# Mixer input, mixer weights and attention tiles moved to one place mod 256 bytes

## The chip, the cores and the metric

The kernel runs on one core of one Trainium2 chip. The metric is the device time of one execution in microseconds. The time before is 871.11 us, the median of 3 runs (870.56 to 871.52).

## The reference

One decoder layer on x of 512 tokens by 1024 features, float32:

```
h = RMSNorm(x)
[q | k | v | x_rnn | g_rnn | gate_attn | gate_rnn] = h @ W_in      (seven blocks of 1024 columns)
A = differential attention(q, k, v)    8 heads, two maps of 64 features each, v of 128, causal,
                                       q and k normalised, a bias by relative distance
R = GeLU(g_rnn) * RG-LRU(CausalConv4(x_rnn))
x = x + (sigmoid(gate_attn) * (A @ P_attn) + sigmoid(gate_rnn) * (R @ P_rnn)) @ W_out
x = x + relu(RMSNorm(x) @ W_up)^2 @ W_down                         (4096 hidden features)
```

## The kernel before

**Three products for one.** Every large product is done on TensorE in the type float32r, with each operand split into a high part and the rest. `mm3` (lines 135 to 138) issues three matmuls: high x high, high x low, low x high. Each has its own weight load (LDWEIGHTS) of the standing operand, 128 columns; the moving operand streams 512 or 256 columns. The traces list these three as L136, L137 and L138.

**Two shapes.** Feature-major products (`cols_proj`) hold weights as the standing operand and stream 512 tokens of an activation; one unit of weights, 4 x 128 rows by 256 columns, gives 24 matmuls. The gates, x_rnn, g_rnn, the attention's and the recurrent branch's projections, W_out and W_up are done this way. Token-major products (`tok_proj`) hold 128 tokens of the activation `hT` as the standing operand and stream 256 weight columns; q, k and v are done this way, 1152 matmuls in all. The down projection (line 1153) also streams 256 columns: the squared-ReLU activations `us` are moving, the weights standing.

**Where operands lie.** A place here is the address of an operand's first element within its partition, mod 256 bytes. The steps that a product takes inside a tile (128 or 256 or 512 columns of 4 bytes) are multiples of 256 bytes, so a tile's place is that of all its pieces. The places follow from the allocation of the pools, in the order of the code:

| operand | tile and pool | place before |
|---|---|---|
| h, split (`hT`) | one tile of the pool `hp`, left side | 64 |
| h before its norm, split (`hu`), used by the first gate units | pool `p1` | 128 |
| weights `whi`, `wlo` | pool `wp`, buffers of 1024 + 64 elements starting at 64; `weight_pair(shift)` starts the weights `shift` bytes in | 64 + shift |
| q and k transposed, gates, attention output `aT` (`unit`) | pool `actp`, right side, 16 buffers | 224 |
| attention's transposed probabilities `pt`, and v | pool `wk` | 128; 64 or 192 |
| RG-LRU inputs `xh`, `xl`, their block weights `gw`, output `R` | pool `rp` | 128 |
| merged activation (`mT`), in the buffer of `hT` | pool `hp` | 64 |
| second norm's output `h2T` | pool `fin` | 128 |
| `us` | pools `hp` and `fin` | 64 |

The shifts are given when the weights are queued (lines 238 to 257): 0 for the gates, x_rnn, g_rnn and W_out (weights at 64), 64 for q, k, v, P_rnn and W_up (at 128; W_down too), 160 for P_attn (at 224).

**Stages.** The order of TensorE's work is written out by generators that are interleaved by cost (`fill_in`, `chain`, `tick`). First (to about 41 us) the input is normed and the first gate units are computed from `hu`. From 41 to 228 us q, k and v of four pairs of heads are computed token-major, with steps of the attention (logits at line 531, transposes at 483 and 565, products with v at 136 to 138) set between them. From 228 to 308 us the rest of the attention is interleaved with gate units on `hT`. From 308 to 448 us two streams alternate: x_rnn and g_rnn units on `hT` (through `wb`), each followed by the RG-LRU's elementwise work and six block-diagonal products on `xh` and `xl` per tile, and, by `fill_in` in `tick`, P_attn's units on `aT` (through `wa`). Then R @ P_rnn (to 490 us), W_out on `mT` (to 533 us), and the MLP, where W_up and a seven-product form of W_down alternate.

**What feeds it.** Weights come by DMA from SP's queue into raw buffers; ScalarE casts the high part (`A.copy(hi, raw)`), VectorE subtracts for the low part. ScalarE, VectorE and GpSimd each run in the order of the program (`InOrder`). The `wa` and `wb` lists fetch and cast a unit or two ahead.

Of the kernel before, what the change touches and what calls it, by code (L numbers as in the profile page):

```python
# [11 lines left out]
F32 = mybir.dt.float32  # L12
F32R = mybir.dt.float32r
# [6 lines left out]
P = 128  # L20
S = 512
DM = 1024
NT = S // P
KT = DM // P
# [13 lines left out]
def tile_block(ctx: ExitStack, tc: tile.TileContext, x, w_in, w_rga, w_rgx, w_pa, w_pr, w_o,  # L38
# [6 lines left out]
    hp = ctx.enter_context(tc.tile_pool(name="hp", bufs=1))  # L45
# [168 lines left out]
        V.tensor_scalar(out=t, in0=ss, scalar1=1.0 / n, scalar2=EPS, op0=ALU.mult, op1=ALU.add)  # L214
        G.tensor_tensor(out=dst, in0=t, in1=mhalf[:, :width], op=ALU.pow)

    hT = hp.tile([P, 2, KT, S], F32R, tag="hT", name="hT")
    hT = [hT[:, j] for j in range(2)]

    smt = cp.tile([P, NSM], F32, name="smt")  # L220

# [15 lines left out]

    OQ, OK_, OV, OX, OG, OGA, OGR = (j * DM for j in range(7))
    wa = Weights(2, 2)
    wa.cols(w_in, OGA + 512)  # L240
    for j in range(4):
        for o in (OQ, OK_, OV):
            wa.cols(w_in, o + 256 * j, 64)
    wa.cols(w_in, OGA + 768)
    for j in range(4):
        wa.cols(w_in, OGR + 256 * j)
    for j in range(4):
        wa.cols(w_pa, 256 * j, 160)
    wb = Weights(1, 1)
    for j in range(4):  # L250
        wb.cols(w_in, OX + 256 * j).cols(w_in, OG + 256 * j)
    for u in range(2):
        for j in range(2):
            wb.cols(w_pr, 256 * j, 64, 4 * u, 4)
# [4 lines left out]
    R, aT, mT = [None] * KT, [None] * NH, [None] * KT  # L259
    tgr, tga = [None] * KT, [None] * KT  # L260
    es_act = ExitStack()
    actp = es_act.enter_context(tc.tile_pool(name="actp", bufs=16, side="right", reuse_waits="tile"))

    def unit(name, dt=F32R):
# [556 lines left out]
    with tc.tile_pool(name="rp", bufs=1, reuse_waits="tile") as rp:  # L821
        fill = chain(ga, y_attn())
        side = []
# [284 lines left out]
    for n, (kind, a, p, pairs) in enumerate(steps):  # L1108
        o = kind, a, p
# [35 lines left out]
        k = seen.get(o, 0)  # L1145
# [58 lines left out]
```

## Time and profile before

| | |
|---|---|
| median of 3 runs | 871.11 us |
| profiled execution | 871.49 us, of which the span is 869.7 us |
| mean granted TensorE clock | 0.999 |
| TensorE busy | 864.0 us, 99% of the span, 5239 matmuls |
| VectorE, ScalarE, GpSimd busy | 602.2, 427.3, 64.3 us |
| DMA | 99.28 MB, 114 GB/s on average |

In the views below, PE is TensorE's matmuls and PEld its weight loads, DVE is VectorE, ACT ScalarE, SP the queue of SyncE. A row of a timeline gives the start in us, the length in us, the engine, the line, the operation, and output <- inputs; starts are counted from the start of the span. Matmuls are pipelined and overlap, so the distance between two starts is the pace, not the length of one. A row of groups gives the number of instructions, then their busy time and the mean length of one in ns, then the idle time before them. A row of the chain of waits gives start, length and what held the chain.

### The profile page before, as it was taken

The numbers are of one execution on the slowest core, as the hardware profiler recorded it, in microseconds if no ns is written. First come the engines' busy times: TensorE is split into PE (matmuls) and PEld (weight loads), VectorE is DVE, ScalarE is ACT, GpSimd is POOL, SyncE is SP. The second block draws the span as 40 slices with busy tenths as digits, with TensorE's granted clock in tenths as the row PEclk, the third lists the DMA queues.
The fourth block names the chain that finished last, engine by engine and source line by source line (L and its number), as shares of the span: only waits on it lengthen the run. The fifth ranks groups of instructions, "written<-read, shape, count | busy, mean of one in ns | idle before, by whom it ended". The sixth has DMA issues, their size and how long they took to land.

```text
span 869.7 us, 13211 instructions
## 1 busy us (share of the span) xinstructions
PE 864.0 (99%) x5239; PEld 759.0 (87%) x5239; DVE 602.2 (69%) x1052; ACT 427.3 (49%) x679; POOL 64.3 (7%) x71
## 2 busy tenths in 40 slices
PE   9999999999999999999999999999999999999998
PEld 7899999999888888888888888888988998899898
DVE  6765688887866346968876656777846775667577
ACT  7444355454545327576663234556335544544341
POOL 0030222113011100000000000000000000000000
PEclk9999999999999999999999999999999999999999
DMA  5358222121321442322213633323652364246354
GB/s 200 116 167 241 87 64 77 58 90 62 101 70 38 114 141 97 101 93 97 73 49 121 228 136 103 115 76 79 160 195 73 98 171 144 73 124 191 86 135 122
DMA packets 33118, 99.28 MB, mean 114 GB/s; under 512 B 3984, under 2 KB 8792, under 8 KB 33056
## 3 DMA queue, kind: packets, MB, share of 16 engines
q1 hardware_dynamic: 29856, 87.93, 30.7%
q0 software_dynamic: 3200, 10.50, 6.2%
q8 instruction: 41, 0.67, 0.3%
q14 instruction: 21, 0.17, 0.1%
HBM read 87.89 MB, written 4.76 MB: 107 GB/s over the span
## 4 chain that ended last, share of the span: by engine, by line
PE 92%; DVE 3%; DMA 2%; ACT 2%; issue 1%; SPq 0%
PE acc L136 22%; PE acc L138 21%; PE acc L137 21%; PE acc L1153 18%; PE at L531 2%; PE at L137 2%; PE at L138 2%; PE at L136 2%; DVE wlo L66 1%; PE at L565 1%; ACT whi L66 1%; PE at L483 1%; PE at L596 1%; DMA wraw<-in_w_in_dram 1%; DMA xT<-in_x_dram 1%; DVE pe L66 1%
## 5 line engine op out<-in xcount | busy, mean ns | idle before, releaser
L1153 PE MATMUL acc<-us,whi 128*128 128x256 f32 x896 | 157.7, 280 | 0.0
L66 DVE TENSOR_TENSOR wlo<-wraw,whi 128x1024 fp32r<-128x1024 f32 (+2 forms) x86 | 96.9, 1148 | 73.2 <-ACT whi L66 73.1
L66 ACT CAST whi<-raw 128x1024 fp32r<-128x1024 f32 x88 | 90.6, 1049 | 101.9 <-DVE raw L66 41.6
L1153 PEld LDWEIGHTS acc<-us,whi 128*128 128x128 f32 x896 | 136.8, 188 | 0.4
L1153 PE MATMUL acc<-us,wlo 128*128 128x256 f32 x448 | 125.6, 280 | 0.0
L66 DVE TENSOR_TENSOR wlo<-raw,whi 128x1024 fp32r<-128x1024 f32 x88 | 106.5, 1218 | 15.8 <-ACT whi L66 15.7
L136 PE MATMUL acc<-whi,hT 128*128 128x256 f32 x384 | 110.2, 287 | 0.0
L137 PE MATMUL acc<-wlo,hT 128*128 128x256 f32 x384 | 107.6, 280 | 0.1
L138 PE MATMUL acc<-whi,hT 128*128 128x256 f32 x384 | 107.4, 280 | 0.0
L66 ACT CAST whi<-wraw 128x1024 fp32r<-128x1024 f32 (+2 forms) x86 | 82.5, 981 | 42.3 <-DMA wraw<-in_w_in_dram 24.5
L136 PE MATMUL acc<-h2T,whi 128*128 128x512 f32 x256 | 99.7, 389 | 0.0
L138 PE MATMUL acc<-h2T,wlo 128*128 128x512 f32 x256 | 99.7, 389 | 0.0
L137 PE MATMUL acc<-h2T,whi 128*128 128x512 f32 x256 | 99.7, 389 | 0.0
L1153 PEld LDWEIGHTS acc<-us,wlo 128*128 128x128 f32 x448 | 85.7, 191 | 0.0
L136 PE MATMUL acc<-hT,whi 128*128 128x512 f32 x208 | 82.4, 396 | 0.0
L138 PE MATMUL acc<-hT,wlo 128*128 128x512 f32 x208 | 81.8, 393 | 0.1
L137 PE MATMUL acc<-hT,whi 128*128 128x512 f32 x208 | 81.5, 392 | 0.0
L136 PEld LDWEIGHTS acc<-whi,hT 128*128 128x128 f32 x384 | 72.1, 188 | 4.3 <-issue 3.0
L137 PEld LDWEIGHTS acc<-wlo,hT 128*128 128x128 f32 x384 | 72.1, 188 | 0.9 <-issue 0.5
L138 PEld LDWEIGHTS acc<-whi,hT 128*128 128x128 f32 x384 | 72.2, 188 | 0.6 <-issue 0.4
L66 ACT ACTIVATE pe<-pe,nm 128x128 f32<-128x128 f32 (+3 forms) x64 | 35.5, 556 | 65.9 <-DVE nm L66 65.9
L66 DVE TENSOR_TENSOR x<-acc,x 128x512 f32<-128x512 f32 (+1 forms) x52 | 33.2, 645 | 40.4 <-PE acc L1153 31.0
(192 smaller groups left out, 1607.3 us busy)
## 6 DMA issues: line engine op xcount, KB each, us to landing
wraw<-in_w_in_dram SPq DMA_DIRECT2D x54, 512.0 KB, 3.5
raw<-in_w_up_dram SPq DMA_DIRECT2D x32, 512.0 KB, 4.2
raw<-in_w_dn_dram SPq DMA_DIRECT2D x32, 512.0 KB, 3.4
raw<-raw POOLq DMA_DIRECT2D x16, 512.0 KB, 4.6
wraw<-in_w_pa_dram SPq DMA_DIRECT2D x8, 512.0 KB, 4.3
wraw<-in_w_pr_dram SPq DMA_DIRECT2D x8, 512.0 KB, 3.5
wraw<-in_w_o_dram SPq DMA_DIRECT2D x8, 512.0 KB, 3.4
trep<-tdram SPq DMA_DIRECT2D x8, 320.0 KB, 4.8
```

The costliest lines, as they stand in the source:

```text
L66: ins = f(*a, **k)
L136: T.matmul(o, l[0], r[0], start=first, stop=False)
L137: T.matmul(o, l[0], r[1], start=False, stop=False)
L138: T.matmul(o, l[1], r[0], start=False, stop=last)
L483: T.transpose(out=ps[:, t * P:(t + 1) * P], in_=qn[t // 2][:, c0:c0 + P], identity=ident)
L531: T.matmul(lg[c][:, :N], qT[r, x0, i * P:(i + 1) * P], kT[r, y0, :N], start=a == 0, stop=a == 2)
L565: T.transpose(out=tp[:, b * P:(b + 1) * P], in_=st[s][:, b * P:(b + 1) * P], identity=ident)
L596: T.matmul(ps[:, t:t + 1], sq[:, t * P:(t + 1) * P], ones, start=True, stop=True)
L1153: T.matmul(d, l[:, i, P * u:P * u + P], act[:, r, f, i % 2], start=p in ("M1", "M2", "M5") and k == z == e == 0 and (u == 0 or isinstance( ...
```

## The change

`hT` gets a tile 64 elements longer and starts 16 elements (64 bytes) into it: its place goes from 64 to 128. The gates', x_rnn's and g_rnn's weights get shift 64 (place 128 instead of 64), P_attn's shift 64 instead of 160 (128 instead of 224), and the weights of q, k and v shift 0 (64 instead of 128). A tile of 24 elements (96 bytes), never used, is allocated ahead of the right-side pool, so that all its buffers move from 224 to 128. Nothing else is edited: no instruction is added, removed or moved.

So the feature-major products on `hT` and on `aT` have both operands at 128 (before: both at 64, and both at 224), the first gate units on `hu` have both at 128 (before: moving 128, standing 64), the logits both at 128 (before: both at 224), and the token-major products have moving at 64 and standing at 128 (before: 128 and 64). R, `mT`, the MLP and v keep their places.

```
-    hT = hp.tile([P, 2, KT, S], F32R, tag="hT", name="hT")
-    hT = [hT[:, j] for j in range(2)]
+    hT = hp.tile([P, 2 * KT * S + 64], F32R, tag="hT", name="hT")
+    hT = [hT[:, 16 + j * KT * S:16 + (j + 1) * KT * S].rearrange("p (k s) -> p k s", k=KT) for j in range(2)]
...
     wa = Weights(2, 2)
-    wa.cols(w_in, OGA + 512)
+    wa.cols(w_in, OGA + 512, 64)
     for j in range(4):
         for o in (OQ, OK_, OV):
-            wa.cols(w_in, o + 256 * j, 64)
-    wa.cols(w_in, OGA + 768)
+            wa.cols(w_in, o + 256 * j)
+    wa.cols(w_in, OGA + 768, 64)
     for j in range(4):
-        wa.cols(w_in, OGR + 256 * j)
+        wa.cols(w_in, OGR + 256 * j, 64)
     for j in range(4):
-        wa.cols(w_pa, 256 * j, 160)
+        wa.cols(w_pa, 256 * j, 64)
     wb = Weights(1, 1)
     for j in range(4):
-        wb.cols(w_in, OX + 256 * j).cols(w_in, OG + 256 * j)
+        wb.cols(w_in, OX + 256 * j, 64).cols(w_in, OG + 256 * j, 64)
...
     es_act = ExitStack()
+    es_act.enter_context(tc.tile_pool(name="pad", bufs=1, side="right")).tile([P, 24], F32, name="pad")
     actp = es_act.enter_context(tc.tile_pool(name="actp", bufs=16, side="right", reuse_waits="tile"))
```

## The prediction

> **What bounds the kernel now.** The page comes first, then the chain of waits.
>
> ```profile
> span 869.7 us, 13211 instructions
> PE 864.0 (99%) x5239; PEld 759.0 (87%) x5239; DVE 602.2 (69%) x1052; ACT 427.3 (49%) x679; POOL 64.3 (7%) x71
> PE 92%; DVE 3%; DMA 2%; ACT 2%; issue 1%; SPq 0%
> ```
>
> TensorE is busy for 99% of the span and holds 92% of the chain. The other engines end the work in two places only, as the longest pieces of the chain show:
>
> ```profile
> 41.79 1.14 DVE wlo L66
> 42.98 0.39 PE acc L137
> ...
> 291.66 0.24 PE acc L138
> ...
> 308.85 1.24 DVE wlo L66
> 310.13 0.50 PE acc L138
> ...
> 599.83 39.57 PE acc L1153 x336
> 682.92 39.57 PE acc L1153 x336
> ```
>
> Up to 43 us VectorE is in front, and from 291.7 to 310.1 a chain of casts and weight loads runs beside a TensorE that is still fed. From there to the output every long piece is a matmul. So the kernel's time is the sum of the distances between starts of matmuls. The durations of matmuls do not say that, since they overlap; I work with starts.
>
> The order of instructions is the same before and after. Only addresses change, so the question is whether a product's pace depends on them. The places (address within a partition, mod 256 bytes) follow from the allocation: hT starts at 64, the tiles of the right pool (q and k transposed, gates, aT) at 224, a weight buffer at 64 plus its shift, hence at 64, 128 or 224. R, h2T and the block-diagonal gate products (xh, xl, gw) are at 128 with their weights, mT and its weights at 64.
>
> The stretches below show the weight loads, one for each product, so that their number is the number of products:
>
> ```profile
> core 0: us, PEld busy (x), PEclk, DMA share, GB/s
> 308.09:448.09 140.00, 113.83 (x608) 1.00 0.30 96
> 450.39:489.83 39.44, 32.66 (x175) 1.00 0.34 111
> 490.74:533.36 42.62, 35.29 (x188) 1.00 0.46 159
> 79.18:84.60 5.42, 5.42 (x47) 1.00 0.83 236
> 66.67:74.49 7.82, 7.82 (x70) 1.00 0.73 213
> ```
>
> The first three hold products of 512 columns only. In the second everything is at 128: its first and last starts lie 174 products apart, 39.44 / 174 = 226.7 ns. The third is all at 64: 42.62 / 188 = 226.7 ns. So 64 and 128 are equally good, as long as both operands stay there. The first stretch interleaves three places: hT (64), aT (224), xh and xl (128). It takes 140.00 / 607 = 230.6 ns a product (one of the 608 loads belongs to the product after the edge), at a granted clock of 1.00 in all rows. The groups of that stretch show the same:
>
> ```profile
> L138 PE MATMUL acc<-hT,wlo 128*128 128x512 f32 x121 | 47.8, 395 | 0.1
> L137 PE MATMUL acc<-aT,whi 128*128 128x512 f32 x64 | 25.2, 394 | 0.0
> L138 PE MATMUL acc<-R,wlo 128*128 128x512 f32 x64 | 24.6, 390 | 0.0
> L138 PE MATMUL acc<-mT,wlo 128*128 128x512 f32 x64 | 24.9, 389 | 0.0
> ```
>
> Where the extra time sits can be read from single starts:
>
> ```profile
> 313.92 0.40 PE L136 MATMUL acc<-hT,whi 128*128 128x512 f32 x1
> ...
> 316.00 0.39 PE L136 MATMUL acc<-hT,whi 128*128 128x512 f32 x1
> ...
> 318.05 0.39 PE L136 MATMUL acc<-aT,whi 128*128 128x512 f32 x1
> ...
> 319.44 0.40 PE L136 MATMUL acc<-hT,whi 128*128 128x512 f32 x1
> ...
> 340.14 0.39 PE L136 MATMUL acc<-hT,whi 128*128 128x512 f32 x1
> ...
> 341.50 0.39 PE L136 MATMUL at<-xh,gw 128*128 128x512 f32 x1
> ...
> 342.88 0.40 PE L136 MATMUL acc<-aT,whi 128*128 128x512 f32 x1
> ```
>
> After a change from aT to hT the first nine products (313.92 to 316.00) take 2.08 us, 231 ns each; the next nine (to 318.05) take 2.05, 228 with the last one, during which the weights of the other place are already loaded. The six of aT (to 319.44) take 1.39, 232 each. Before 341.50 hT has settled: six in 1.36, 227 each. The six xh and xl that follow take 1.38, 230 each. So a change of place upsets the pace for some nine products, and then it settles at 226.7. A new tile at the same place does not: R takes another tile every six products, and its 39.44 us hold no such trace.
>
> **The change part by part.** The sum is made against the profiled execution: 871.49 us (span 869.7), 0.38 over the median of the runs, 871.11.
>
> *The interleaved stretch, 308 to 448 us.* With hT, its weights, aT, its weights and xh, xl, gw all at 128, there is no change of place until R gives way to mT. At the settled pace 607 products take 607 x 0.2267 = 137.6 us, 2.4 less than the 140.0 measured. Part of that is a wait for weights:
>
> ```profile
> 309.44 0.40 PE L136 MATMUL acc<-hT,whi 128*128 128x512 f32 x1
> 309.67 0.40 PE L137 MATMUL acc<-hT,whi 128*128 128x512 f32 x1
> 310.13 0.50 PE L138 MATMUL acc<-hT,wlo 128*128 128x512 f32 x1
> 310.46 0.40 PE L136 MATMUL acc<-hT,whi 128*128 128x512 f32 x1
> ```
>
> The two steps from 309.67 to 310.46 are 0.79 us where two products take 0.45: 0.34 is the wait, which ends with the cast at 308.85 + 1.24 and stays. That leaves 2.07, and I leave 0.07 for the products upset by this wait and by the gate products' own waits: **-2.0 us**. Its bounds are 0, if it is not the place that upsets the pace, and -2.1. What could swallow it is the feed of weights running late; the chain names no cast and no load between 310.13 and the end, and each unit of 24 products gives the feed only 0.08 us less.
>
> *hT between steps of the attention, 230 to 289 us.* Here hT is interrupted by logits (place 224 on both operands), transposes and products with v. The first products after an interruption are upset as well:
>
> ```profile
> 242.40 0.39 PE L137 MATMUL acc<-hT,whi 128*128 128x512 f32 x1
> ...
> 247.43 0.40 PE L138 MATMUL acc<-hT,wlo 128*128 128x512 f32 x1
> ```
>
> These are 22 steps in 5.03 us, 0.04 over the settled pace. There are some thirteen such runs; the starts of all 168 products of them, without the first of each run, add up to 0.4 over. The logits come to 128 like hT, but transposes and v do not move, and short products break the pace by their length alone. Between nothing and 0.4 I take **-0.15**; the other bound is +0.4, as much again, if entries come out worse.
>
> *Token-major products, 41 to 228 us: 1152 of 256 columns.* Moving goes from 128 to 64, standing from 64 to 128. Before, they run at two paces: 5.42 / 46 = 117.8 ns from 79.18, and 7.82 / 69 = 113.3 ns from 66.67, each kept until an interruption. Counting starts through the stage, about 900 products go at the slower pace and 190 at the faster, and some 50 border on other work. The down projection already has the new places, moving 64 and standing 128: the chain's 336 in 39.57 us are 117.8 ns, the same. In its last stretch it too finds the faster pace:
>
> ```profile
> 827.35 38.85 PE acc L1153 x336
> ```
>
> That is 0.72 less than 39.57 in the chain's count. So swapping the places changes neither pace as far as rows show; which of the two a run falls into may be drawn anew. I take **0**. The bounds are 900 x 4.5 ns = -4.0 us, all runs fast, and 190 x 4.5 = +0.9, all runs slow.
>
> *The first gate unit on hu, 30 to 41 us.* Moving 128 on weights at 64 become both 128. Its 48 products cost at most 2 ns more than settled, about 0.1 us, but VectorE is in front up to 41.79 + 1.14. So **0**; without that cover -0.1.
>
> *Logits, 192 products.* Both operands go from 224 to 128, equal before and after. **0**; no row shows logits elsewhere, so the bound is the 4 ns between 230.6 and 226.7 on each, about 0.8 us either way.
>
> *Casts and copies* write to other places. Weight casts for shift 64 and shift 0 take the same, so **0**:
>
> ```profile
> L66 DVE TENSOR_TENSOR wlo<-wraw,whi 128x1024 fp32r<-128x1024 f32 x18 | 21.6, 1223 | 9.4 <-ACT whi L66 9.3
> L66 DVE TENSOR_TENSOR wlo<-wraw,whi 128x1024 fp32r<-128x1024 f32 x15 | 18.2, 1223 | 14.2 <-ACT whi L66 14.2
> ```
>
> The first row is 60 to 220 us (shift 64 before), the second 340 to 428 us (mostly shift 0). No instruction, DMA or wait is added. The larger tiles shift the left pools by 256 bytes and the right one by 96, so two load buffers of the MLP overlap one right-hand tile each where they overlapped two; their first loads may start earlier, beside a TensorE that does not wait there: 0.
>
> The sum: 871.49 - 2.0 - 0.15 = 869.34; taken to the median (-0.38) 868.96, so **869.0 us**.
>
> **The rivals.**
>
> *No effect.* The places do not matter, and what upsets the pace is the switch between two interleaved streams, each with its accumulators; or the pad does not move the right pool, and aT stays at 224 while its weights go to 128. For it: 64 against 224 always coincides with such a switch. Against it: the two streams of the first part of the R stretch also alternate weights and accumulators, at 226.7; and from R to mT (one stream ending) the pace is upset too. It gives 871.1. The Trainium skill's "TensorE: Matmul & The Clock Gate" (Step-by-step: what each phase is for) would decide for this rival: the moving operand and the weight load have independent read ports, so that loading the next weights takes nothing from the running matmul. The trace does not bear it out as far as it goes: 230.6 against 226.7 ns with the same shapes, engines and clock.
>
> *Token-major becomes faster.* hT's standing place then agrees with that of the logits, gates and attention's moving tiles, and more runs enter the faster pace. For it: the paces are 4.5 ns apart and 900 products stand to gain. Against: the down projection, with these very places, starts both quoted stretches at the slower one. At half of the 4.0 us: 867.0.
>
> *Token-major becomes slower*, and the kernel with it. In the attention, products of 256 columns with standing 64 above moving, as token-major will have, can go slower than either pace:
>
> ```profile
> 276.74 0.28 PE L136 MATMUL at<-pt,v 128*128 128x256 f32 x1
> ...
> 277.46 0.49 PE L565 MATMUL at<-ident,pe 128*128 128x128 f32 x3
> ```
>
> Six in 0.72 us are 120 ns. If token-major, chopped by the same interruptions, went at that pace, 1100 products would cost 120 - 117 = 3 ns more than their present mean of 117.0: +3.3, less 2.15, so 1.15 us slower than before, 872.3. It decides the sign from 2.15 / 1100 = 2 ns more a product, 119 ns. Against it: these six border on other work at both ends, and the down projection's long stretches show no such pace.
>
> **How the numbers follow.** Forecast 0.62, no effect 0.16, token-major faster 0.14, slower 0.08. What a measurement of this kernel can tell from no change is about 0.2%, 1.74 us: below 869.37 is faster. The forecast lies only 0.4 below that line, and its own range is 868.1 to 869.9 (the bounds of the attention's runs, and half the spread of the runs, 0.5, added); I give it 0.7 of lying below. Faster: 0.62 x 0.7 + 0.14 = 0.57. Slower by over 0.2% needs over 872.85, most of the last rival's reach and more: 0.05. Within: 0.38. The range goes down to 866.6, past half of token-major's gain, and up to 871.1, no effect; about 0.06 lies below and 0.14 above.
>
> **What would show it.** Right: in the stretch from the first aT to the last one, products start 226.7 to 227.2 ns apart, the stretch is about 138 us long, and the groups on hT and aT come to 389 or 390 ns like R's. The runs of hT between attention steps would still be upset in part. Token-major would again show two paces, 113.3 and 117.8, with some fifth or less at the faster one. Wrong: pace still upset at each change from hT to aT; waits of matmuls for casts after 310 us; a mean pace of token-major outside 116.5 to 117.5 ns; or a stage that the change does not touch (MLP, from 533 us) that differs by over half a microsecond.

## The result and the profile after

The changed kernel takes 867.1 us (median of 6 runs, 866.98 to 868.17) against 871.2 us before: a ratio of 0.995, 95% interval 0.994 to 0.996. The profiled execution takes 867.03 us, its span is 865.3 us, 4.4 less than before. The page says at first sight what it said before, TensorE holding the chain:

```profile
PE 859.6 (99%) x5239; PEld 756.8 (87%) x5239; DVE 602.1 (70%) x1052; ACT 427.1 (49%) x679; POOL 64.3 (7%) x71
PE 93%; DVE 4%; ACT 2%; DMA 1%; issue 1%; SPq 0%
```

The instructions are the same and in the same order, so the two traces can be cut at the same products. The windows begin at the first token-major product, at the first interleaved product after the last of these, at the first on `aT`, at the first product after the last on `aT`, and at the first of W_up. In each row stand the window, its length, the busy time and number of weight loads, the granted clock, the DMA share and GB/s; first before, then after:

```profile
41.23:228.00 186.77, 174.53 (x1543) 1.00 0.34 106
228.00:308.05 80.05, 65.52 (x422) 1.00 0.28 83
308.05:448.08 140.03, 113.86 (x607) 1.00 0.30 96
448.08:533.58 85.50, 70.77 (x377) 1.00 0.40 135
533.58:866.00 332.42, 301.84 (x2113) 1.00 0.43 123
```

```profile
41.24:226.08 184.84, 172.45 (x1543) 1.00 0.35 107
226.08:306.13 80.05, 65.48 (x422) 1.00 0.28 83
306.13:443.71 137.58, 113.93 (x607) 1.00 0.30 98
443.71:529.18 85.47, 70.76 (x378) 1.00 0.40 134
529.18:861.60 332.42, 301.79 (x2113) 1.00 0.43 123
```

Two stages moved and no other: the interleaved stretch by 2.45 us, the token-major stage by 1.93. The start, the rest of the attention, R @ P_rnn with W_out, and the MLP agree to 0.03 us.

In the interleaved stretch 607 products now take 137.58 us, 226.7 ns each, and the groups have the length that R and `mT` had:

```profile
L138 PE MATMUL acc<-hT,wlo 128*128 128x512 f32 x121 | 47.1, 389 | 0.0
L137 PE MATMUL acc<-aT,whi 128*128 128x512 f32 x64 | 24.9, 389 | 0.0
```

The first products after a change from `aT` to `hT`, and the six on `aT` after them, no longer show that anything changed:

```profile
311.57 0.39 PE L136 MATMUL acc<-hT,whi 128*128 128x512 f32 x1
...
313.61 0.39 PE L136 MATMUL acc<-hT,whi 128*128 128x512 f32 x1
...
315.65 0.39 PE L136 MATMUL acc<-aT,whi 128*128 128x512 f32 x1
...
317.01 0.39 PE L136 MATMUL acc<-hT,whi 128*128 128x512 f32 x1
```

Nine in 2.04 us, nine in 2.04, six in 1.36: all 227 ns, where before the same pieces took 2.08, 2.05 and 1.39.

In the token-major stage the two paces are still there, 113.4 and 117.8 ns, but their shares have turned round. Of the 1152 products, counted by the distance to the next start, 198 were fast (115 ns or less) and 905 slow before; 747 are fast and 349 slow after; the rest border on other work. That is 549 x 4.4 ns = 2.4 us; 0.5 us of it went to the products next to other work, whose first steps became a little longer.

### The profile page after: what moved, and what is told of

Same layout as the page of the kernel before. It is cut to its first block, busy times and chain, and to the rows that moved or that the text cites. A ratio compares the mean times of both kernels' runs of the same rounds, so it can differ in the third digit from the quotient of the medians.

```text
span 865.3 us, 13211 instructions
## 1 busy us (share of the span) xinstructions
PE 859.6 (99%) x5239; PEld 756.8 (87%) x5239; DVE 602.1 (70%) x1052; ACT 427.1 (49%) x679; POOL 64.3 (7%) x71
## 4 chain that ended last, share of the span: by engine, by line
PE 93%; DVE 4%; ACT 2%; DMA 1%; issue 1%; SPq 0%
PE acc L136 22%; PE acc L137 22%; PE acc L138 22%; PE acc L1154 18%; PE at L532 2%; PE at L137 2%; PE at L136 2%; PE at L138 2%; PE at L566 1%; DVE wlo L66 1%; DVE pe L66 1%; PE at L484 1%; PE at L597 1%; ACT pe L66 1%; DMA xT<-in_x_dram 1%
```

## The experiments

The stages lie apart in time, so one run's trace can answer two questions. Windows of weight loads are shown as above.

**The kernel before, once more.** No edit.

> The kernel before, unchanged, in another execution. If the paces are set by the program: token-major again has about 17% of its products at the fast pace and a mean of 117.0 ns, and the stretch of hT and aT about 2.1 us over the settled pace, without the wait of 0.34 us if that was a late weight transfer. If they are drawn in each execution: a share well off 17%.

It took 871.08 us in one run. The token-major stage and the interleaved stretch:

```profile
41.38:227.90 186.52, 174.28 (x1544) 1.00 0.34 106
308.00:447.70 139.70, 113.91 (x607) 1.00 0.30 96
```

247 of the 1152 products were fast, 21%, and the mean pace of the undisturbed ones was 116.8 ns. That is near 17% and 117.0, so the share goes with the program, though not to the last product. The stretch is 0.33 shorter than in the first profile, the wait of 0.34 us at 310 being absent; it is 2.1 over 137.6.

**Attention tiles and P_attn's weights at 128, `hT` at 64.**

```
+    es_act.enter_context(tc.tile_pool(name="pad", bufs=1, side="right")).tile([P, 24], F32, name="pad")
...
-        wa.cols(w_pa, 256 * j, 160)
+        wa.cols(w_pa, 256 * j, 64)
```

> The kernel before with one edit: the right-side tiles and P_attn's weights move from 224 to 128; hT and its weights stay at 64, token-major stays moving 128, standing 64. Theory (any change between places mod 256 upsets the pace of products of 512 columns): hT at 64 and aT at 128 still differ, the stretch from the first aT to the last stays at 139.5 to 140.0 us, time 871 (870.3 to 871.6). Rival (only places that are not multiples of 64 bytes upset it, as 224 is): the stretch comes to about 137.7 us and the time to about 868.9. In both, token-major keeps a mean pace near 117.0 ns.

It took 869.92 us, ratio 0.9984 (0.9974 to 0.9994). Both theories missed, each by half:

```profile
41.37:227.99 186.62, 174.67 (x1543) 1.00 0.33 106
307.91:446.72 138.81, 113.94 (x607) 1.00 0.30 97
```

```profile
313.42 0.39 PE L136 MATMUL acc<-hT,whi 128*128 128x512 f32 x1
...
314.80 0.39 PE L136 MATMUL acc<-hT,whi 128*128 128x512 f32 x1
...
317.52 0.39 PE L136 MATMUL acc<-aT,whi 128*128 128x512 f32 x1
```

Six products in 1.38 us after the change of place are upset (230 ns), the twelve after them take 2.72, settled at 226.7. Before, the upset lasted nine. So a change between 64 and 128 upsets the pace as well, but for a shorter time than one to 224: the stretch stands 1.2 us over 137.6 where it stood 2.1 over. Token-major did not move (172 fast products), though the logits now lay at 128.

**Attention tiles and P_attn's weights at 64, where `hT` already was.**

```
+    es_act.enter_context(tc.tile_pool(name="pad", bufs=1, side="right")).tile([P, 40], F32, name="pad")
...
-        wa.cols(w_pa, 256 * j, 160)
+        wa.cols(w_pa, 256 * j)
```

> The kernel before with the right-side tiles and P_attn's weights moved to 64, where hT and its weights already are; token-major stays moving 128, standing 64. Theory (one place for the interleaved streams is what counts, whichever it is): the stretch from first to last aT loses 1.5 to 2.0 us (only xh and xl at 128 still interrupt), token-major stays near 117.0 ns with about a fifth of its products at the fast pace, time 869.3 to 869.8. Rival (128 itself, not the sameness, is the good place): the stretch stays at 140, time 871.

It took 869.42 us, ratio 0.9978 (0.9968 to 0.9987), within what the theory gave:

```profile
41.90:228.47 186.57, 174.68 (x1544) 1.00 0.34 106
308.46:446.48 138.02, 113.93 (x607) 1.00 0.30 98
```

The stretch is 0.4 over the settled time; what remains are the products on `xh` and `xl`, still at 128. So it is the sameness that counts, not 128. Token-major, with its places of before, kept its length (167 fast products).

**The changed kernel without the pad: `hT` and its weights at 128, token-major swapped, attention tiles at 224.**

```
-    es_act.enter_context(tc.tile_pool(name="pad", bufs=1, side="right")).tile([P, 24], F32, name="pad")
...
-        wa.cols(w_pa, 256 * j, 64)
+        wa.cols(w_pa, 256 * j, 160)
```

> The changed kernel without the pad and with P_attn's weights at 224: right-side tiles at 224 as before, hT and its weights at 128, token-major moving 64, standing 128. Theory A (the pair of places decides how soon token-major finds its fast pace): mean pace 114.9 ns as in the changed kernel, some two thirds of the products fast, 2.2 us less than before in that stage; stretch of hT and aT still 140 us; time 869.0. Theory B (the neighbours' places, logits at 224 or 128, decide): mean pace back near 117.0, time 871.

It took 868.91 us, ratio 0.9971 (0.9959 to 0.9983):

```profile
41.07:225.88 184.81, 172.39 (x1543) 1.00 0.35 107
305.90:445.33 139.43, 113.90 (x607) 1.00 0.29 97
```

Token-major has the whole gain (184.81 against 184.84 with the full change; 748 fast products, mean 114.9 ns) though the logits are back at 224. Theory A stands: the pair of places decides, not the neighbours. The interleaved stretch has next to none of its gain.

**Other distances.** The distance is the standing place less the moving one, mod 256. In this kernel, made from the changed one, the four pairs of heads (q, k and v) and the four chunks of W_down each get a distance of their own:

```
-            wa.cols(w_in, o + 256 * j)
+            wa.cols(w_in, o + 256 * j, 64 * j)
...
-        hi, lo = weight_pair(0 if own else 64, fin if own else None)
+        place = (128, 64, 192, 0)[a[0]] if kind == "dn" else 128
+        hi, lo = weight_pair((place - (128 if own else 64)) % 256, fin if own else None)
```

> The changed kernel with other places for products of 256 columns: q, k and v of the four pairs of heads have moving at 64, 128, 192 and 0 in turn (standing 128), the four chunks of W_down have standing at 128, 64, 192 and 0 in turn (moving 64). Theory (the distance of standing from moving decides, and 64 above is one of the good ones): token-major of the first pair has two thirds at 113 ns; pair 2 (distance 0) and pair 4 (128 above) differ from it, pair 3 (64 below, as before the change) is mostly at 118. In W_down the first chunk stays at 117.8, since it is entered from settled products; another distance may settle at 113.4, which would be worth 1.5 us a chunk of 336. Rival (the entry alone decides): all four pairs show about the same share, all chunks but the last 117.8.

Four windows in token-major with distance 64, 0, -64 and 128 (moving at 64, 128, 192, 0; standing at 128), each from one start to another:

```profile
65.47:70.23 4.76, 4.76 (x43) 1.00 0.76 208
99.02:103.81 4.79, 4.79 (x41) 1.00 0.33 109
161.88:167.29 5.41, 5.41 (x47) 1.00 0.00 0
190.71:196.23 5.52, 5.52 (x47) 1.00 0.00 0
```

They hold 42, 40, 46 and 46 steps: 113.3, 119.8, 117.6 and 120.0 ns. Over all undisturbed products of each pair of heads the means are 114.5, 119.6, 117.6 and 118.9, with 75, 1, 5 and 15% at 115 ns or less. In the changed kernel, with distance 64 throughout, the four pairs have 75, 72, 76 and 48%. The 15% at distance 128 are single steps in a repeating pattern, not a stretch of fast products. W_down's chunks by the chain, with distance 64, 0, 128 and -64:

```profile
597.16 39.57 PE acc L1155 x336
680.25 40.31 PE acc L1155 x336
764.12 39.87 PE acc L1155 x336
825.79 39.84 PE acc L1155 x336
```

Per product 117.8, 120.0 and 118.7 ns; the last holds a wait, its products go at 117.8. So the distance matters, and W_down at distance 64, entered from settled products, does not find the fast pace. That another distance might settle at 113.4 did not come out: none did so by itself. In this trace long fast stretches stand at distance 64 alone, but -64 has them too, only more rarely: the 70 products from 66.67 us of the kernel before, shown in the prediction, went at 113.3 ns. The one run took 870.96 us.

**W_down 64 bytes further.** Moving at 128, standing at 192:

```
-            t = t if n % 3 == 0 else t[:, 48:48 + 7168]
+            t = t[:, 16:16 + 7168] if n % 3 == 0 else t[:, :7168]
...
-        hi, lo = weight_pair(0 if own else 64, fin if own else None)
+        up = 64 if kind == "dn" else 0
+        hi, lo = weight_pair(up + (0 if own else 64), fin if own else None)
```

> The changed kernel with the down projection's operands both 64 bytes further: moving at 128, standing at 192. The distance of 64 stays, the entry changes: in the settled W_up products before it both operands are at 128, so now the moving place stays at the entry and the standing one jumps. Theory (distance 64 has two paces, 113.4 and 117.8 ns, and the entry chooses): the long stretches, now 336 in 39.57 us, may come to 38.1 us each; all four would take 4.9 us off, time 862. If the entry chooses the slow pace again: 867.1, no stretch changes. Rival (the places themselves, 64 and 128, make the two paces): another pace than both appears.

```profile
596.05 39.58 PE acc L1155 x336
679.17 39.58 PE acc L1155 x336
```

No pace other than the two appeared, and the slow one came again in these and the third chunk (39.58 us). The fourth took 39.85 us against 38.83 in the changed kernel: its last 226 products went at 117.8 ns, where those of the changed kernel went at 113.3 after the same interruption. It took 867.47 us, ratio 0.9955 (0.9937 to 0.9972), as the changed kernel.

**A small product ahead of each chunk; 512 columns at other distances.**

```
             banks[a] = [psum("acc") for _ in range(3)]
+            if a[1] == 0:
+                X = banks[a][0]
+                if a[0] == 0:
+                    T.transpose(out=X[:, :P], in_=ident, identity=ident)
+                elif a[0] == 1:
+                    T.matmul(X[:, :P], h2T[0][:, 0, :P], h2T[1][:, 0, :P], start=True, stop=True)
+                elif a[0] == 2:
+                    T.matmul(X[:, :256], h2T[0][:, 0, :P], h2T[1][:, 0, :256], start=True, stop=True)
+                else:
+                    T.matmul(X[:, :64], h2T[0][:, 0, :P], h2T[1][:, 0, :64], start=True, stop=True)
...
-        wb.cols(w_pr, 256 * j, 64)
+        wb.cols(w_pr, 256 * j, (0, 0, 0, 128)[j])
...
-        wb.cols(w_o, 256 * j)
+        wb.cols(w_o, 256 * j, 64 * j)
```

> The changed kernel with one extra small product ahead of each chunk of W_down, its result overwritten: a 128-column float32 transpose (chunk 1), and float32r products of 128, 256 and 64 columns with both operands at 128 (chunks 2, 3, 4); and with the weights' place varied where 512 columns are streamed: the last two quarters of R @ P_rnn at 64 and 192 (moving 128), the quarters of W_out at 64, 128, 192 and 0 (moving 64). Theory: a disturbed entry lets distance 64 fall into the fast pace, as token-major does after transposes; a chunk that does takes about 38.2 us in place of 39.57, less some 0.2 for the extra product. Rival (W_down's pace does not depend on the entry): all chunks at 117.8 and 0.1 to 0.3 us longer. Of 512 columns: distance 0 stays at 226.7 ns, another distance costs 0 to 4 ns a product (the first gate units, 64 below, took 229).

It took 868.05 us in one run. Six windows of one quarter each, 48 products: R @ P_rnn at -64 and 64, W_out at 0, 64, 128 and -64:

```profile
463.82:474.81 10.99, 9.01 (x48) 1.00 0.14 49
474.81:486.01 11.20, 9.02 (x48) 1.00 0.47 151
486.01:496.90 10.89, 9.01 (x48) 1.00 0.89 317
496.90:508.10 11.20, 9.02 (x48) 1.00 0.55 198
508.10:519.26 11.16, 9.04 (x48) 1.00 0.13 49
519.26:530.26 11.00, 9.02 (x49) 1.00 0.29 90
```

That is 229.0, 233.3, 226.9, 233.3, 232.5 and 229.2 ns. For 512 columns distance 0 is best and 64 worst, the reverse of 256 columns; 64 costs up to 6.6 ns a product, beyond the 4 expected. The chunks of W_down:

```profile
596.55 38.10 PE acc L1164 x336
678.24 39.63 PE acc L1164 x336
761.53 39.57 PE acc L1164 x336
```

The first, after the transpose, runs at 113.4 ns from its fourth product to its last. The second and third, after products of 128 and 256 columns, stayed at 117.8, against the theory: not every break does it. The fourth, after the product of 64 columns, began fast as well, until a wait for a weight cast at 834 us threw it back to the slow pace.

**Breaks ahead of chunks 1, 2 and 3.** Four further kernels, from the changed one. First transposes (the edit is shown), then, in a second kernel, two more ahead of the halves of chunk 4:

```
+            if a[1] == 0 and a[0] < 3:
+                T.transpose(out=banks[a][0][:, :P], in_=ident, identity=ident)
```

> The changed kernel with one extra 128-column float32 transpose (of the identity, into a bank that is overwritten) ahead of chunks 1, 2 and 3 of W_down. Theory (distance 64 has two paces and a break in the stream lets it fall into the fast one): each of the three chunks takes 38.4 us with the transpose in place of 39.8 between the last W_up product and the next one, 4.1 us in all, time 863.0 (862.5 to 864). Rival (the one chunk that became fast was luck): one or two chunks stay at 39.7, time 864.5 to 867.3.

> As the run with three transposes, and two more: ahead of chunk 4's first half and of its second half, which begins after a wait for a weight cast has broken the stream. Theory: the first 98 products of chunk 4 gain 0.4 us less 0.15; its second half is already at the fast pace where the wait leaves it so and then loses 0.15, or gains 0.6 where the wait leaves it slow. Time 862.3 to 863.5.

The chunks of the first:

```profile
595.57 38.10 PE acc L1156 x336
677.32 39.58 PE acc L1156 x336
760.52 38.10 PE acc L1156 x336
```

The first took 864.79 us, ratio 0.9924 (0.9911 to 0.9936): the rival's case, two chunks of three. The second took 865.24 us, 0.9930 (0.9916 to 0.9943), above the 862.3 to 863.5 expected: chunk 2 was slow again, the first half of chunk 4 stayed slow up to its wait for weights, and the second half, fast in the changed kernel, became slow behind its transpose. Then the short product, ahead of chunk 2 with the transposes of 1 and 3 kept, or ahead of all three (the edit shown):

```
+            if a[1] == 0 and a[0] < 3:
+                T.matmul(banks[a][0][:, :64], h2T[0][:, 0, :P], h2T[1][:, 0, :64], start=True, stop=True)
```

> The run with three transposes left chunk 2 slow (39.58 us) and made chunks 1 and 3 fast (38.10). Here chunk 2 gets a float32r product of 64 columns in place of the transpose, which made chunk 4's first part fast in an earlier run. Theory (the kind of break chooses the pace): chunk 2 comes to about 38.1 to 38.2 us, time 863.4. Rival (what precedes chunk 2 keeps it slow whatever breaks it): chunk 2 stays at 39.6, time 864.8.

> The changed kernel with a float32r product of 64 columns ahead of chunks 1, 2 and 3 in place of transposes. Theory (this kind of break leads to the fast pace): all three chunks at about 38.1 us, time 863.4. Rival (a break leads to either pace as the start happens to fall): one or two of the three stay at 39.6, time 864.6 to 866.

With transposes ahead of 1 and 3 and the short product ahead of 2, chunk 2 is fast and chunk 3, fast twice after the same transpose, is slow:

```profile
595.94 38.10 PE acc L1158 x336
677.60 38.18 PE acc L1158 x336
759.43 39.58 PE acc L1158 x336
```

With the short product ahead of all three, all three are fast:

```profile
595.96 38.18 PE acc L1156 x336
677.71 38.18 PE acc L1156 x336
759.45 38.18 PE acc L1156 x336
```

The times are 864.93 us, ratio 0.9927 (0.9913 to 0.9940), and 863.37 us, 0.9908 (0.9894 to 0.9921). The last beats both kernels, the one before by 7.9 us beside it, and the changed one by 3.7 between medians. That a break can lead to either pace is shown by the transpose; that the product of 64 columns always leads to the fast one is not: it did so in all five of its places.

## Why the prediction was right or wrong

**What bounds the kernel**: right. All of the gain lies in distances between starts on TensorE, and it was passed on whole: the MLP starts 4.4 us earlier and ends 4.4 us earlier.

**Interleaved stretch, -2.0**: right. It measured -2.45, of which 2.1 is pace and 0.34 the wait that was to stay. That wait was absent when the kernel before ran once more, so this part of the gain is luck. The reason given, that a change of place upsets some nine products, needs one correction: where only 64 and 128 take part the upset is shorter, and the stretch stands 1.2 us over the settled pace in place of 2.1.

**hT between steps of the attention, -0.15**: it measured 0.00 (80.05 and 80.05 us). So small a term could not have been told in one pair of traces: in the others this stage takes 79.9 to 80.3 us. The products of the attention go on breaking the pace where they lie at hT's place. In the changed kernel, after logits with every operand at 128, nine steps take 2.10 us, 233 ns each:

```profile
235.39 0.40 PE L137 MATMUL acc<-hT,whi 128*128 128x512 f32 x1
...
237.49 0.39 PE L137 MATMUL acc<-hT,whi 128*128 128x512 f32 x1
```

The prediction put this to the length of short products alone. That is not shown: the products on hT from 247.90 us are upset as well, and the logits before them stream 512 columns, of 64 rows.

**Token-major, 0**: this step failed. It measured -1.93, almost as much as the change's other half. The prediction said that swapping the places changes neither pace, which is so, said that the share of each pace may be drawn anew, and took no net move, with a fifth or less of the products fast. The share goes with the distance. In the four traces with -64 (the kernel before twice, and the two with only the attention's tiles moved) 14 to 21% of the 1152 products are fast and the stage takes 186.5 to 186.8 us; in the eight with 64 throughout 53 to 66% are fast and it takes 184.5 to 185.2. Inside each group it varies from trace to trace. The prediction named a mean pace outside 116.5 to 117.5 ns as a sign of being wrong, and that sign came: 114.9. W_down, which has distance 64, was read as evidence that 64 is no better. Its chunks are entered from settled products of 512 columns, and entered so their first products went at 117.8 ns in every trace; with some breaks ahead of them the same products go at 113.4 ns. Long runs without interruptions were the wrong witnesses for short ones with many.

**hu, logits, casts, 0 each**: nothing stands against it; the start of the kernel agrees to 0.01 us. The 48 products on `hu` that changed places went from 229.0 to 226.7 ns, 0.1 us that did not reach the next stage. The other 96 on `hu` had both operands at 128 already before.

**The sum.** It came to 869.34 us for the profiled execution, which took 867.03. Of the 2.3 us between, 1.93 is the token-major stage and 0.34 the absent wait. The time lies in the range only because the range had been carried past half of token-major's possible gain; the forecast itself, 869.0, was 1.9 too high.

**The rivals.** No effect is refuted: the streams still switch as before, each with its accumulators, and their products take 226.7 ns. The Trainium skill's "TensorE: Matmul & The Clock Gate" (Step-by-step: what each phase is for) states that loading the next weights takes no read bandwidth from the running matmul. The traces do not agree if that is to make the operands' places indifferent: in one trace the same products take 113.3 ns at distance 64 and 119.8 at 0. Whether reads are what costs the time, no run here shows. The time of the rival "token-major faster", 867.0, is the one that came, 867.1. Its cause is not the one it named: the gain is there in full with the logits at 224. Nor was half of the possible 4.0 us argued for, so that the figure fits is luck. The slower pace of 120 ns that the last rival took from six products of the attention exists, at distance 0 and in part of the products at 128, but not as a lasting pace at 64.

## What to carry to other kernels

When TensorE is the bound and its products stream float32r, read the distance between starts, not the length of matmuls, and compare it between stages of one shape: a few ns in hundreds of products point to where the operands lie. Products that are interleaved should lie at one place mod 256 bytes, with moving and standing operand at the same place where 512 columns stream, and standing 64 bytes above moving where 256 do: these were the best of the four distances tried, for float32r on one core. A stream can sit at a slow pace for as long as nothing breaks it, so a stage that is slow with the right places is no proof against them.

## What the runs showed of the hardware

Pace by distance (standing less moving place, mod 256), from starts at a granted clock of 1.00:

| distance | 256 columns | 512 columns |
|---|---|---|
| 0 | 120.0 ns | 226.7 ns |
| 64 | 113.4 or 117.8, each kept until a break | 233.3 |
| 128 | 118.7 to 120.0 | 232.5 |
| -64 | 117.8 or, more rarely, 113.4, each kept until a break | 229.0 |

The 512-column paces at 64, 128 and -64 come from one run, 48 or 96 products each. The period of 256 bytes is taken for granted here: four distances with four paces show that it is not 128 or less, and no run tests a longer one by itself.

It was not expected that one stream, with the same operands, has two paces and that a single short product, which itself costs some 0.1 us, moves 336 products from one to the other. Why it does, why the transpose ahead of chunk 3 led to both, and why distance 64 enters the fast pace more often than -64, is open: no run here shows the reads themselves.
